# Seven block products in place of eight in a feed-forward layer, with the weight sums on GpSimd

## The chip, the cores and the metric

The kernel runs on one core of a Trainium2 chip. The metric is the device time of one execution, in microseconds (us). A core has TensorE (matmuls into PSUM), VectorE, ScalarE and GpSimd, each with a queue of its own that is worked off in order, and DMA queues that move data between the memory (HBM) and the on-chip SBUF. SBUF and PSUM have 128 partitions; "128x512" is 128 partitions of 512 columns.

## What is computed

One layer: a mixer (a gated delta net and an RWKV7 group), cross attention to a memory, and a feed-forward part, for 256 tokens of width 2048 in float32. The change touches the last part alone:

```python
def squared_relu_mlp(u, w1, w2):
    return jnp.square(jax.nn.relu(u @ w1)) @ w2

# in reference(): w1 is [2048, 8192], w2 is [8192, 2048]
        h = h + squared_relu_mlp(rmsnorm(h, ffn_norm_w[l]), ffn_w1[l], ffn_w2[l])
    return rmsnorm(h, final_norm_w)
```

## The kernel before

Every large product is made of three products of `float32r` parts: an operand x is split into `hi` (a cast, on ScalarE) and `lo = x - hi` (a subtraction, on VectorE), and hi·hi + hi·lo + lo·hi stands for the float32 product. Activations are split once; weights are streamed from HBM, 512 KB at a time, through SP's queue into a ring of five `raw` tiles, and split on the way (`weights`, line 228): `A.copy(hi, w)` on line 239 and the subtraction through the helper on line 110, into three pairs of buffers `whi`/`wlo` (128x512 each).

The feed-forward part (line 1180 on) runs in four chunks `ch` of 2048 hidden columns. In each chunk the first product comes first: `gemm_T` (line 261) computes it transposed, in parts of 128 hidden columns by 256 tokens. A part has 16 k tiles, for each a matmul with a stationary `whi` over 512 columns (both parts of the activations side by side, line 273) and one with `wlo` over 256 columns (line 272 or 275), alternating, all into one PSUM bank. There are 64 such parts. `relu2` then copies one half of the bank (ScalarE), adds the other (VectorE), applies the squared ReLU (VectorE) and splits the result into `fhi` and `flo`.

Then the chunk's second product: `gemm` (line 244), four blocks of 512 output columns, each with 16 k tiles by two halves of the tokens (`m`) by three matmuls of 512 columns (lines 254 to 256). The result is added to `h`, times the squared norm factor `rf`, by `add_ffn` on VectorE. The last block of the last chunk runs one half of the tokens after the other (`gemm_rows`, line 205), so that the first half's final norm (`final`) can go under the second half's matmuls.

GpSimd does nothing in this part but the two powers of the final norm. `tt` (line 110) is `tensor_tensor`, on VectorE unless `e=G` puts it on GpSimd; `stt` (line 113) is `scalar_tensor_tensor` on VectorE. The program's order on each engine is set by a scheduler at build time from the order and priorities of the code; loads and splits of weights have a higher priority.

PSUM has eight banks: three under the tag `g`, two each under `s0` and `s1`, one under `x`. In the feed-forward part only `g` is used.

Of the kernel before, what the change touches and what calls it, by code (L numbers as in the profile page):

```python
# [17 lines left out]
P = 128  # L18
# [22 lines left out]
def host_layout(inp):  # L41
# [32 lines left out]
    def col(v):  # L74
# [22 lines left out]
        "w1": blocks_T(a["ffn_w1"][0]), "w2": blocks(a["ffn_w2"][0]),  # L97
# [7 lines left out]
def body(ctx, tc, I, out, dbg=None, upto=99):  # L105
# [65 lines left out]
    # derived per-channel scalars  # L171
# [15 lines left out]
    def lhs_split(raws, wname, pool, tag):  # L187
        """raw^T (times the norm's weight) split in two float32r parts, four k tiles a tile, as they are asked for."""
# [16 lines left out]
    def gemm_rows(lhs, wblk, evac, kbs, his, los):  # L205
        """the same, the first 128 tokens before the others, from weights that all stay."""
        kbs, w = list(kbs), []
        for m in range(2):
            acc = bank("g")
            for i, kb in enumerate(kbs):  # L210
                if m == 0:
                    with tc.high_priority(3000):
                        raw = wp.tile([P, KB, NB], F32, tag="raw", name=nm("raw"))
                        nc.sync.dma_start(out=raw, in_=wblk[kb])
                        hi, lo = his(), los()
                        A.copy(hi, raw)
                        tt(lo, raw, hi.bitcast(F32), ALU.subtract)
                    w.append((hi, lo))
                hi, lo = w[i]
                for q in range(KB):  # L220
                    first, last = i == 0 and q == 0, i == len(kbs) - 1 and q == KB - 1
                    xh, xo = lhs(kb * KB + q, m)
                    T.matmul(acc, lhsT=xh, rhs=hi[:, q], start=first, stop=False)
                    T.matmul(acc, lhsT=xh, rhs=lo[:, q], start=False, stop=False)
                    T.matmul(acc, lhsT=xo, rhs=hi[:, q], start=False, stop=last)  # L225
            evac(m, acc)

    def weights(src, a, b, parts):
        """a block of weights [128, a, b] in two float32r parts."""
# [14 lines left out]
    def gemm(lhs, wblk, n, evac, kbs=None):  # L244
        """[256 tok, n] = lhs^T @ W: three float32r products stand for the float32 one."""
# [15 lines left out]
    def gemm_T(rhs, wblk, evac):  # L261
        """(x W)^T in four parts of 128 columns, [128 col, (W x_hi, W_hi x_lo)]; rhs(kt) is (x_hi, x_lo)^T, 512 wide."""
        for j in range(4):
            acc = bank("g")
            for b in range(2):
                w = weights(wblk[j, b], 8, P, 2)
                for k in range(8):
                    first, last = b == 0 and k == 0, b == 1 and k == 7
                    x = rhs(8 * b + k)
                    xf = x.rearrange("p a t -> p (a t)")  # L270
                    if not first:
                        T.matmul(acc[:, 0:S], lhsT=w[k][1], rhs=x[:, 0], start=False, stop=False)  # L272
# [26 lines left out]
    def rms(src, name):  # L299
        """1 / rms of the rows of src[:, m, :]."""  # L300
# [60 lines left out]
    # the clock of the array rises and the functions' table loads while the first operands are on their way  # L361
# [73 lines left out]
    # gates of the deltanet: [tok, chunk, head]  # L435
# [35 lines left out]
    inv = [0]  # L471

    def inverse(B, pool, pool2):
        """B is overwritten with the inverse of I + (its strictly upper part); what lies below its diagonal is zero.

        X12 = -X11 B12 X22 for blocks of 2 to 128, the larger ones on tiles of the array."""
# [11 lines left out]
        def quarters(t, n):  # L488
            """the quarters 11, 12, 22 of the diagonal blocks of 2n: [q, block, row, column]."""
# [94 lines left out]
    def rw_shift(pt, c0, names, blks):  # L584
        """columns c0.. of the projection [tok, col] to shifted [col, tok] tiles of two blocks."""
# [12 lines left out]
    def rw_unit(u, r, k, v):  # L598
# [59 lines left out]
        # bonus * v  # L658
# [8 lines left out]
        # scores  # L667
# [21 lines left out]
        # [tok, .] forms  # L689
# [57 lines left out]
        # group norm, bonus, gate  # L747
# [94 lines left out]
    def dn_unit(g, kq, v2):  # L842
# [6 lines left out]
        # norms per token: [tok, (k/q), chunk, head]  # L849
# [21 lines left out]
        # decays, scores  # L871
# [72 lines left out]
        # norm over the head, times silu(z)  # L944
# [90 lines left out]
    def tok_T(src, wname):  # L1035
        """transposes of src [tok, 2048] (times the norm's weight), split in two parts, four k tiles a step."""
# [85 lines left out]
    def low():  # L1122
        for _ in range(2):
            t = da.tile([P, 2, KB, NB], F32R, tag="kq", bufs=2, name=nm("llo"))
            yield t[:, 0]
            yield t[:, 1]
        for _ in range(4):
            yield fp.tile([P, KB, NB], F32R, tag="llo", bufs=4, name=nm("llo"))

    def high():  # L1130
        for _ in range(4):
            t = lx.tile([P, 2, KB, NB], F32R, tag="lx", name=nm("lhi"))
            yield t[:, 0]
            yield t[:, 1]

    llo, lhi = low(), high()

    def final(m):
        ss = part[:, m, 7:8]
        stt(ss, part[:, m, 4:5], 1.0 / D, part[:, m, 6:7], ALU.mult, ALU.add)  # L1140
        ro = small.tile([P, 1], F32, tag="ro", name=nm("ro"))
        power(ro, ss, -0.5, 1)
        for q in range(4):
            d = h[:, m, q * NB:(q + 1) * NB]
            if q == 3:
                stt(d, d, ro, fw[:, q * NB:], ALU.mult, ALU.mult)
            elif q:
                act(d, d, AF.Copy, scale=ro)
            else:
                ts(d, d, ro, ALU.mult)  # L1150
            (A if q % 2 else nc.sync).dma_start(out=out[m * P:(m + 1) * P, q * NB:(q + 1) * NB], in_=d)

    def add_ffn(gcol):
        def f(m, p):
            d = h[:, m, gcol * NB:(gcol + 1) * NB]
            stt(d, p, rf[:, m:m + 1], d, ALU.mult, ALU.add)
        return f

    def last_h(gcol):
        def f(m, p):  # L1160
            sl = slice(gcol * NB, (gcol + 1) * NB)
            d = h[:, m, sl]
            stt(d, p, rf[:, m:m + 1], d, ALU.mult, ALU.add)
            rms_part(h, part, m, gcol)
            tt(d, d, fw[:, sl], ALU.mult)
        return f

    def last(m, p):
        """the last 512 columns in two halves, so that little is left to do once the second's sum of squares is there."""
        V.tensor_reduce(part[:, m, 5:6], part[:, m, 0:3], axis=AX.X, op=ALU.add)  # L1170
        ts(part[:, m, 5:6], part[:, m, 5:6], 1.0 / D, ALU.mult, EPS, ALU.add)
        for i in range(2):
            d = h[:, m, 3 * NB + i * S:3 * NB + (i + 1) * S]
            stt(d, p[:, i * S:(i + 1) * S], rf[:, m:m + 1], d, ALU.mult, ALU.add)
            junk = ptp.tile([P, S], F32, tag="pt", name=nm("junk"))
            act(junk, d, AF.Square, accum=part[:, m, 3 + i:4 + i])
# [48 lines left out]
```

## Time and profile before

| | |
|---|---|
| median of 3 runs | 1446.87 us (1446.61 to 1447.17) |
| span of the profiled execution | 1442.5 us |
| TensorE busy | 1414.8 us, 98% |
| VectorE busy | 950.1 us, 66% |
| ScalarE busy | 780.8 us, 54% |
| GpSimd busy | 50.6 us, 4% |
| DMA | 252.88 MB, mean 175 GB/s |

The runs' time contains the span and some 4 us around it. Busy times are shares of the span. Matmuls are pipelined: the next starts before the one ahead has ended, and the ends are modelled, so a matmul's price is the distance from its start to the next one's. The same holds to a smaller degree for VectorE.

### The profile page before, as it was taken

The numbers are of one execution on the slowest core, as the hardware profiler recorded it, in microseconds if no ns is written. First come the engines' busy times: TensorE is split into PE (matmuls) and PEld (weight loads), VectorE is DVE, ScalarE is ACT, GpSimd is POOL, SyncE is SP. The second block draws the span as 40 slices with busy tenths as digits, with TensorE's granted clock in tenths as the row PEclk, the third lists the DMA queues.
The fourth block names the chain that finished last, engine by engine and source line by source line (L and its number), as shares of the span: only waits on it lengthen the run. The fifth ranks groups of instructions, "written<-read, shape, count | busy, mean of one in ns | idle before, by whom it ended". The sixth has DMA issues, their size and how long they took to land.

```text
span 1442.5 us, 22496 instructions
## 1 busy us (share of the span) xinstructions
PE 1414.8 (98%) x8284; PEld 1168.9 (81%) x8284; DVE 950.1 (66%) x1799; ACT 780.8 (54%) x1491; POOL 50.6 (4%) x66
## 2 busy tenths in 40 slices
PE   9999999999999989999999999999999999999997
PEld 7877788787876868887788888888888888888886
DVE  7748574869587685767676655666556665566664
ACT  7656454555456454566565544555445554455553
POOL 0010001100010000000000000000000000000000
PEclk9999999999999999999999999999999999999999
DMA  7444433454366464556465556555665555655554
GB/s 281 157 145 152 135 121 112 147 177 144 102 200 207 138 190 146 166 173 212 136 209 186 190 192 197 185 187 189 193 197 186 185 190 194 195 182 187 191 188 146
DMA packets 90688, 252.88 MB, mean 175 GB/s; under 512 B 20673, under 2 KB 29393, under 8 KB 90193
## 3 DMA queue, kind: packets, MB, share of 16 engines
q1 hardware_dynamic: 70304, 243.96, 51.2%
q10 hardware_dynamic: 19920, 6.42, 1.8%
q8 instruction: 65, 1.06, 0.3%
q0 software_dynamic: 352, 1.06, 0.2%
q14 instruction: 47, 0.38, 0.1%
HBM read 244.72 MB, written 6.69 MB: 174 GB/s over the span
## 4 chain that ended last, share of the span: by engine, by line
PE 82%; DMA 7%; DVE 6%; ACT 3%; issue 2%; SPq 0%; POOL 0%; ACTq 0%; POOLq 0%; DVEq 0%
PE ps_g L273 16%; PE ps_g L255 16%; PE ps_g L254 15%; PE ps_g L256 15%; PE ps_g L272 8%; DVE wlo L110 2%; PE ps_s L675 2%; DMA scr<-Sc 1%; DMA xc<-inv 1%; DMA mraw<-in_memT_dram 1%; PE ps_x L312 1%; DMA g<-scr 1%; DVE xtmp L110 1%; DMA junk<-in_mem_dram 1%; PE ps_s L312 1%
## 5 line engine op out<-in xcount | busy, mean ns | idle before, releaser
L110 DVE TENSOR_TENSOR wlo<-raw,whi 128x512 fp32r<-128x512 f32 x848 | 583.3, 691 | 388.1 <-ACT whi L239 386.8
L239 ACT CAST whi<-raw 128x512 fp32r<-128x512 f32 x848 | 523.4, 621 | 489.8 <-DVE wlo L110 203.7
L273 PE MATMUL ps_g<-hhl,whi 128*128 128x512 f32 x1024 | 357.6, 398 | 0.2 <-ACT whi L239 0.2
L272 PE MATMUL ps_g<-hhl,wlo 128*128 128x256 f32 x960 | 269.9, 281 | 0.0
L273 PEld LDWEIGHTS ps_g<-hhl,whi 128*128 128x128 f32 x1024 | 188.4, 188 | 42.5 <-ACT whi L239 0.5
L255 PE MATMUL ps_g<-wlo,xhl 128*128 128x512 f32 x512 | 209.9, 410 | 8.4 <-DVE wlo L110 8.3
L256 PE MATMUL ps_g<-whi,xhl 128*128 128x512 f32 x512 | 202.0, 395 | 0.0
L256 PE MATMUL ps_g<-whi,flo 128*128 128x512 f32 x480 | 186.7, 389 | 0.0
L255 PE MATMUL ps_g<-wlo,fhi 128*128 128x512 f32 x480 | 186.7, 389 | 0.0
L254 PE MATMUL ps_g<-whi,xhl 128*128 128x512 f32 x512 | 180.8, 406 | 3.4 <-ACT whi L239 3.4
L272 PEld LDWEIGHTS ps_g<-hhl,wlo 128*128 128x128 f32 x960 | 181.5, 189 | 2.8 <-ACT hhl L122 0.2
L254 PE MATMUL ps_g<-whi,fhi 128*128 128x512 f32 x480 | 151.3, 389 | 0.0
L255 PEld LDWEIGHTS ps_g<-wlo,xhl 128*128 128x128 f32 x512 | 96.6, 189 | 37.7 <-DVE wlo L110 18.2
L254 PEld LDWEIGHTS ps_g<-whi,xhl 128*128 128x128 f32 x512 | 94.6, 189 | 26.7 <-ACT whi L239 5.9
L256 PEld LDWEIGHTS ps_g<-whi,xhl 128*128 128x128 f32 x512 | 96.7, 189 | 18.8 <-issue 0.7
L255 PEld LDWEIGHTS ps_g<-wlo,fhi 128*128 128x128 f32 x480 | 90.1, 188 | 18.8
L256 PEld LDWEIGHTS ps_g<-whi,flo 128*128 128x128 f32 x480 | 90.1, 188 | 18.7
L254 PEld LDWEIGHTS ps_g<-whi,fhi 128*128 128x128 f32 x480 | 90.1, 188 | 18.6
L113 DVE SCALAR_TENSOR_TENSOR cy<-ps_x,colt,cy 128x255 f32<-128x255 f32 (+2 forms) x72 | 34.2, 476 | 10.9 <-ACT cy L122 10.3
L1191 ACT CAST fhi<-hid 128x256 fp32r<-128x256 f32 x64 | 26.1, 408 | 9.5 <-DVE hid L113 0.8
L113 DVE SCALAR_TENSOR_TENSOR hid<-hid 128x256 f32<-128x256 f32 x64 | 27.2, 425 | 2.2
L113 DVE SCALAR_TENSOR_TENSOR h<-ps_g,rf,h 128x512 f32<-128x512 f32 (+1 forms) x34 | 22.8, 712 | 8.0 <-PE ps_g L225 8.0
(360 smaller groups left out, 1540.7 us busy)
## 6 DMA issues: line engine op xcount, KB each, us to landing
raw<-in_w_dram SPq DMA_DIRECT2D x256, 512.0 KB, 3.5
raw<-in_w_in_dram SPq DMA_DIRECT2D x112, 512.0 KB, 3.5
raw<-in_w_out_dram SPq DMA_DIRECT2D x32, 512.0 KB, 3.5
raw<-in_wk_dram SPq DMA_DIRECT2D x8, 512.0 KB, 3.5
mraw<-in_memT_dram SPq DMA_DIRECT2D x8, 512.0 KB, 3.6
raw<-in_wq_dram SPq DMA_DIRECT2D x8, 512.0 KB, 3.4
raw<-in_wv_dram SPq DMA_DIRECT2D x8, 512.0 KB, 3.7
raw<-in_wo_dram SPq DMA_DIRECT2D x8, 512.0 KB, 3.5
```

Source lines behind the costliest of these rows:

```text
L110: return (e or V).tensor_tensor(o, a, b, op=op)
L113: return V.scalar_tensor_tensor(o, a, s, b, op0=op0, op1=op1)
L239: A.copy(hi, w)
L254: T.matmul(acc[m][:, :n], lhsT=xh, rhs=w[q][0], start=first, stop=False)
L255: T.matmul(acc[m][:, :n], lhsT=xh, rhs=w[q][1], start=False, stop=False)
L256: T.matmul(acc[m][:, :n], lhsT=xl, rhs=w[q][0], start=False, stop=last)
L272: T.matmul(acc[:, 0:S], lhsT=w[k][1], rhs=x[:, 0], start=False, stop=False)
L273: T.matmul(acc, lhsT=w[k][0], rhs=xf, start=first, stop=last)
L312: T.transpose(out=o[:, j * P:(j + 1) * P], in_=a, identity=ident)
L675: T.matmul(bb[hl][:, 256 * i:256 * i + 256], lhsT=BK[hs, j, i, cs], rhs=AR[hs, j, :, cs], start=True, stop=True)
L1191: A.copy(hi[:, j], t)
```

## The change

The second product is cut into quads. A quad is 256 tokens by 256 hidden columns by 1024 output columns, a 2x2 by 2x2 product of blocks of 128x128 and 128x512. Eight block products would give its four output blocks; the Strassen-Winograd scheme takes seven, from sums and differences of blocks. With three matmuls each a quad has 21 matmuls of 512 columns, not 24. There are 64 quads (16 groups `g` of 512 hidden columns, two halves `q`, two halves `p` of the output).

- Left operands (`lefts`): for each group, four sums of 128x256 on GpSimd, then two casts and two subtractions (768 and 1024 columns) into seven blocks.
- Right operands (`rights`): one 1 MB load (two buffers), then three instructions on GpSimd (1024, 512 and 512 columns; each depends on the one ahead), and three casts and three subtractions (1536, 1024 and 1024 columns) into single buffers `bs`, `bt` and `bu`.
- Seven PSUM banks collect the seven products over a visit (a run of quads with the same `p`; there are nine). At its end `add_products` combines them into `h`: a copy on ScalarE and eleven operations of 512 columns on VectorE.
- The first product keeps its 64 parts, but 8 of them come first and the other 56 follow one quad each; they use the single bank `x`. Within a part the eight `hi` matmuls of a half come before its eight `lo` matmuls.
- The final norm is spread over the last two visits. `gemm_rows` goes.

```diff
+    def quads(w):
+        b = w.reshape(w.shape[0] // 512, 2, 2, P, w.shape[1] // 1024, 2, NB)
+        b = b.transpose(0, 2, 4, 3, 1, 5, 6).reshape(-1, 2, w.shape[1] // 1024, P, 4, NB)
+        return np.ascontiguousarray(b[:, :, :, :, [1, 0, 3, 2]])
...
-    def gemm_T(rhs, wblk, evac):
-        for j in range(4):
-            acc = bank("g")
+    def gemm_T(rhs, wblk, evac, js=range(4), tag="g"):
+        for j in js:
+            acc = bank(tag)
             for b in range(2):
                 w = weights(wblk[j, b], 8, P, 2)
                 for k in range(8):
...
+                    T.matmul(acc, lhsT=w[k][0], rhs=rhs(8 * b + k).rearrange("p a t -> p (a t)"),
+                             start=b == 0 and k == 0, stop=False)
+                for k in range(8):
+                    T.matmul(acc[:, 0:S], lhsT=w[k][1], rhs=rhs(8 * b + k)[:, 0], start=False,
+                             stop=b == 1 and k == 7)
             evac(j, acc)
...
-    fp = ctx.enter_context(tc.tile_pool(name="fp", bufs=5, reuse_waits="tile"))
-    fw = fp.tile([P, D], F32, name="fw", bufs=1)
-    A.dma_start(out=fw, in_=I["fnw"].to_broadcast([P, D]))
+    fp = ctx.enter_context(tc.tile_pool(name="fp", bufs=1, reuse_waits="tile"))
...
+    def relu2(base):
+        def f(j, p):
+            t = da.tile([P, S], F32, tag="cy", bufs=2, name=nm("hid"))
+            A.copy(t, p[:, S:])
+            tt(t, p[:, 0:S], t, ALU.add)
+            t2 = t.rearrange("p (a t) -> p a t", a=2)
+            stt(base[:, 2 * (j // 2):2 * (j // 2) + 2, j % 2], t2, 0.0, t2, ALU.max, ALU.mult)
+        return f
+
+    def lefts(g, base):
+        sm_ = fp.tile([P, 4, 2, P], F32, tag="sm", name=nm("sm"))
+        tt(sm_[:, 0], base[:, 0], base[:, 2], ALU.add, e=G)
+        tt(sm_[:, 1], sm_[:, 0], base[:, 1], ALU.subtract, e=G)
+        tt(sm_[:, 2], base[:, 0], base[:, 1], ALU.subtract, e=G)
+        tt(sm_[:, 3], base[:, 3], sm_[:, 1], ALU.subtract, e=G)
+        hi = fp.tile([P, 7, 2, P], F32R, tag="ahi", bufs=3, name=nm("ahi"))
+        lo = fp.tile([P, 7, 2, P], F32R, tag="alo", bufs=3, name=nm("alo"))
+        A.copy(hi[:, 0:3], base[:, 1:4])
+        tt(lo[:, 0:3], base[:, 1:4], hi[:, 0:3].bitcast(F32), ALU.subtract)
+        A.copy(hi[:, 3:7], sm_)
+        tt(lo[:, 3:7], sm_, hi[:, 3:7].bitcast(F32), ALU.subtract)
+        left[g] = (hi, lo)
+
+    def split(src, n, tag):
+        hi = fp.tile([P, n, NB], F32R, tag=tag + "h", name=nm(tag))
+        lo = fp.tile([P, n, NB], F32R, tag=tag + "l", name=nm(tag))
+        A.copy(hi, src)
+        tt(lo, src, hi.bitcast(F32), ALU.subtract)
+        return [(hi[:, i], lo[:, i]) for i in range(n)]
+
+    def rights(src):
+        with tc.high_priority(3000):
+            raw = da.tile([P, 4, NB], F32, tag="kq", bufs=2, name=nm("rawq"))
+            nc.sync.dma_start(out=raw, in_=src)
+            t13 = wp.tile([P, 2, NB], F32, tag="raw", name=nm("t13"))
+            tt(t13, raw[:, 0].unsqueeze(1).to_broadcast([P, 2, NB]), raw[:, 1:3], ALU.subtract, e=G)
+            t24 = wp.tile([P, 2, NB], F32, tag="raw", name=nm("t24"))
+            tt(t24[:, 0], raw[:, 2], t13[:, 0], ALU.subtract, e=G)
+            tt(t24[:, 1], raw[:, 3], t24[:, 0], ALU.subtract, e=G)
+            b11, b22, b21 = split(raw[:, 1:4], 3, "bs")
+            t1, t3 = split(t13, 2, "bt")
+            t2, t4 = split(t24, 2, "bu")
+        return {1: b11, 2: b21, 3: b22, 4: t4, 5: t1, 6: t2, 7: t3}
...
+    def quad(g, q, p, acc, first, last, order, done):
+        r = rights(I["w2"][g, q, p])
+        hi, lo = left[g]
+        for n in order:
+            xh, xl_ = hi[:, LHS[n], q], lo[:, LHS[n], q]
+            T.matmul(acc[n], lhsT=xh, rhs=r[n][0], start=first, stop=False)
+            T.matmul(acc[n], lhsT=xh, rhs=r[n][1], start=False, stop=False)
+            T.matmul(acc[n], lhsT=xl_, rhs=r[n][0], start=False, stop=last)
+            if last:
+                done(n)
...
+        def add(m, c, x):
+            d = h[:, m, 1024 * p + NB * c:1024 * p + NB * (c + 1)]
+            stt(d, x, rf[:, m:m + 1], d, ALU.mult, ALU.add)
...
+    jblock(8)
+    A.dma_start(out=fw, in_=I["fnw"].to_broadcast([P, D]))
+    for v, (p, gs) in enumerate(visits):
+        acc = [None] + [bank(t) for t in ("g", "g", "g", "s0", "s0", "s1", "s1")]
+        after = {len(visits) - 1: after_last, len(visits) - 2: lambda m, c: early(m, 2 + c, c)}.get(v)
+        done = add_products(p, acc, after)
+        for g in gs:
+            for q in range(2):
+                end = g == gs[-1] and q == 1
+                order = (1, 2, 3, 5, 6, 7, 4) if end else (1, 2, 3, 5, 7, 6, 4)
+                quad(g, q, p, acc, g == gs[0] and q == 0, end, order, done)
+                jblock()
```

## Rows read from the trace of the kernel before

**Rows 1.** The page's first part: busy us, share of the span, instructions.

```profile
PE 1414.8 (98%) x8284; PEld 1168.9 (81%) x8284; DVE 950.1 (66%) x1799; ACT 780.8 (54%) x1491; POOL 50.6 (4%) x66
```

**Rows 2.** Feed-forward stage: busy time by engine (instructions), granted clock, DMA share, GB/s.

```profile
728.00:1442.50 714.50, 706.14 (x3561) 598.46 (x3560) 443.22 (x750) 367.00 (x656) 1.80 (x3) 1.00 0.57 187
```

**Rows 3.** Waits, 780 to 1400 us: who waited for whom, total us, times, longest.

```profile
DVE wlo L110 <- ACT whi L239: 233.4, 366, 1.0
...
ACT whi L239 <- PE ps_g L273: 91.8, 166, 0.8
```

**Rows 4.** Timeline of TensorE, both products: start us, us, engine, line, operation.

```profile
800.87 0.40 PE L273 MATMUL ps_g<-hhl,whi 128*128 128x512 f32 x1
...
806.52 0.40 PE L273 MATMUL ps_g<-hhl,whi 128*128 128x512 f32 x1
...
824.40 0.62 PE L254 MATMUL ps_g<-whi,fhi 128*128 128x512 f32 x2
...
825.76 0.62 PE L254 MATMUL ps_g<-whi,fhi 128*128 128x512 f32 x2
```

**Rows 5.** Timeline of TensorE, first stage: five matmuls of 272 columns.

```profile
16.22 0.29 PE L404 MATMUL ps_s<-whi,xhl 128*128 128x272 f32 x1
...
16.72 0.41 PE L402 MATMUL ps_s<-whi,xhl 128*128 128x272 f32 x2
```

**Rows 6.** ScalarE's groups by shape, feed-forward stage: busy us, mean ns, idle before.

```profile
L239 ACT CAST whi<-raw 128x512 fp32r<-128x512 f32 x492 | 305.8, 622 | 314.4 <-DVE wlo L110 178.5 <-PE ps_g L273 106.2 <-PE ps_g L256 29.1
...
L216 ACT CAST lhi<-raw 128x1024 fp32r<-128x1024 f32 x8 | 8.4, 1050 | 5.5 <-DMA raw<-in_w_dram 5.5
```

**Rows 7.** VectorE's groups by shape, the same stage and columns.

```profile
L110 DVE TENSOR_TENSOR wlo<-raw,whi 128x512 fp32r<-128x512 f32 x492 | 340.2, 692 | 249.7 <-ACT whi L239 249.6
L113 DVE SCALAR_TENSOR_TENSOR hid<-hid 128x256 f32<-128x256 f32 x64 | 27.2, 425 | 2.2
...
L113 DVE SCALAR_TENSOR_TENSOR h<-ps_g,rf,h 128x512 f32<-128x512 f32 x30 | 21.0, 743 | 0.0
L110 DVE TENSOR_TENSOR llo<-raw,lhi 128x1024 fp32r<-128x1024 f32 x8 | 9.7, 1223 | 4.4 <-ACT lhi L216 4.4
```

**Rows 8.** Timeline of VectorE, two instructions back to back.

```profile
805.85 0.69 DVE L110 TENSOR_TENSOR wlo<-raw,whi 128x512 fp32r<-128x512 f32 x1
806.46 0.42 DVE L110 TENSOR_TENSOR flo<-hid,fhi 128x256 fp32r<-128x256 f32 x1
```

**Rows 9.** GpSimd's groups by shape, whole span.

```profile
L682 POOL TENSOR_SCALAR_AFFINE_SELECT Sc<-Sc 128x512 f32<-128x512 f32 x32 | 20.5, 640 | 167.9 <-ACT Sc L680 159.3 <-issue 8.2 <-PE ps_g L256 0.4
...
L1214 POOL MEMSET const-float32-0.0<- 128x1 f32 x1 | 0.1, 100 | 0.3 <-issue 0.3
```

**Rows 10.** Timelines of GpSimd and VectorE where their instructions overlap.

```profile
419.50 0.64 POOL L880 TENSOR_SCALAR_AFFINE_SELECT Dm<-Dm 128x512 f32<-128x512 f32 x1 [1.01 <-ACT Dm L122]
419.68 1.00 DVE L110 TENSOR_TENSOR wlo<-raw,whi 128x512 fp32r<-128x512 f32 x1
...
412.68 0.68 DVE L110 TENSOR_TENSOR wlo<-raw,whi 128x512 fp32r<-128x512 f32 x1
412.90 0.95 POOL L880 TENSOR_SCALAR_AFFINE_SELECT Dm<-Dm 128x512 f32<-128x512 f32 x1 [1.01 <-ACT Dm L122]
413.54 0.85 DVE L110 TENSOR_TENSOR wlo<-raw,whi 128x512 fp32r<-128x512 f32 x1
...
292.50 1.28 POOL L682 TENSOR_SCALAR_AFFINE_SELECT Sc<-Sc 128x512 f32<-128x512 f32 x2 [4.10 <-ACT Sc L680]
292.56 0.75 DVE L117 TENSOR_SCALAR pt<-ps_g,rx 128x512 f32<-128x512 f32 x1 [1.14 <-PE ps_g L256]
```

**Rows 11.** The same, beside a power of 8 columns on GpSimd.

```profile
341.05 2.02 POOL L110 TENSOR_TENSOR rs<-vr,pw 128x8 f32<-128x8 f32 x1 [39.07 <-DVE vr L118]
...
341.84 0.68 DVE L110 TENSOR_TENSOR wlo<-raw,whi 128x512 fp32r<-128x512 f32 x1
```

**Rows 12.** Timeline of TensorE: its last matmul.

```profile
1433.96 0.39 PE L225 MATMUL ps_g<-lhi,flo 128*128 128x512 f32 x1
```

More of the change, by code (lines that the diff above doesn't have):

```diff
@@ L203, in lhs_split @@
         return get
-    def gemm_rows(lhs, wblk, evac, kbs, his, los):
-        kbs, w = list(kbs), []
-        for m in range(2):
-            acc = bank("g")
[L210 to L226, printed above, removed]
     def weights(src, a, b, parts):
@@ L1130, in high @@
[L1130 to L1140, printed above, removed]
+    A11, A22, A12, S1, S2, S3, S4 = range(7)
+    left = {}
+    def relu2(base):
[6 more added lines that the diff above has]
+        return f
@@ new lines, in add_products, with tmp, both, done @@
+    def add_products(p, acc, after=None):
+        def add(m, c, x):
+            d = h[:, m, 1024 * p + NB * c:1024 * p + NB * (c + 1)]
+            stt(d, x, rf[:, m:m + 1], d, ALU.mult, ALU.add)
+        u = {}
+        def tmp(n):
+            u[n] = ptp.tile([P, NB], F32, tag="pt", name=nm("u"))
+            return u[n]
+        def both():
+            if 6 in u and 7 in have and 8 not in u:
+                tt(tmp(8), acc[7], u[6], ALU.add)
+                add(0, 1, u[8])
+                if after:
+                    after(0, 1)
+                add(0, 0, u[8])
+        have = set()
+        def done(n):
+            have.add(n)
+            if n == 1:
+                A.copy(tmp(1), acc[1])
+                add(1, 0, acc[1])
+            elif n == 2:
+                add(1, 0, acc[2])
+                if after:
+                    after(1, 0)
+            elif n == 3:
+                add(1, 1, acc[3])
+            elif n == 5:
+                add(1, 1, acc[5])
+                add(0, 1, acc[5])
+            elif n == 6:
+                tt(tmp(6), acc[6], u[1], ALU.add)
+                add(1, 1, u[6])
+                if after:
+                    after(1, 1)
+                both()
+            elif n == 7:
+                both()
+            elif n == 4:
+                add(0, 0, acc[4])
+                if after:
+                    after(0, 0)
+        return done
@@ new lines, in body, with square_sum @@
+    visits = []
+    for i in range(8):
+        for p in ((0, 1) if i % 2 == 0 else (1, 0)):
+            if visits and visits[-1][0] == p:
+                visits[-1][1].extend((2 * i, 2 * i + 1))
+            else:
+                visits.append((p, [2 * i, 2 * i + 1]))
+    fw = fp.tile([P, D], F32, name="fw")
+    def square_sum(m, c, slot):
+        junk = ptp.tile([P, NB], F32, tag="pt", name=nm("junk"))
+        act(junk, h[:, m, c * NB:(c + 1) * NB], AF.Square, accum=part[:, m, slot:slot + 1])
@@ L1153, in add_ffn @@
[L1153 to L1176, printed above, removed]
-        stt(part[:, m, 6:7], part[:, m, 3:4], 1.0 / D, part[:, m, 5:6], ALU.mult, ALU.add)
-        final(m)
@@ L1180, in body @@
[L1180 to L1204 removed]
+            if k == 0:
+                stt(d, d, ro, fw[:, q * NB:(q + 1) * NB], ALU.mult, ALU.mult)
+            elif k == 1:
+                ts(d, d, ro, ALU.mult)
+            else:
+                act(d, d, AF.Copy, scale=ro)
@@ new lines, in after_last, with jblock @@
+            (A if k % 2 else nc.sync).dma_start(out=out[m * P:(m + 1) * P, q * NB:(q + 1) * NB], in_=d)
+    bases = {}
+    nj = [0]
+    def jblock(n=1):
+        for _ in range(n):
+            if nj[0] == 64:
+                return
+            g, j = divmod(nj[0], 4)
+            if j == 0:
+                bases[g] = da.tile([P, 4, 2, P], F32, tag="v2", name=nm("base"))
+            gemm_T(hl, I["w1"][g], relu2(bases[g]), js=(j,), tag="g" if nj[0] < 8 else "x")
+            if j == 3:
+                lefts(g, bases[g])
+            nj[0] += 1
```

63 lines of the change are left out of this document (16 added, 47 removed).

## The prediction

> **What bounds the kernel now.** I read the page's busy shares first: TensorE 98% of the span [rows 1]. A busy TensorE row says little by itself, since the ends of matmuls are modelled, so I then took the feed-forward stage alone, in the table of busy times by stretch: from 728 us to the end TensorE is busy 706 of 714.5 us at granted clock 1.00, the upper level of 2.4 GHz, VectorE 443, ScalarE 367, GpSimd 1.8 [rows 2]. In the list of waits VectorE waits 233.4 us for ScalarE's casts, and ScalarE waits for buffers that TensorE still reads [rows 3]; TensorE waits for nobody there. So its own pace sets the time, and I read that from the timeline, from start to start and not from durations. In the second product six matmuls of 512 columns start in 1.36 us (824.40 to 825.76), 0.2267 us each; in the first product sixteen pairs of 512 and 256 columns take 5.65 us (800.87 to 806.52) [rows 4]. The stage is 64 such parts of the first product and 64 x 24 matmuls of the second: 64 x (5.65 + 24 x 0.2267 = 5.44) = 64 x 11.09 = 710 us, and that is the stage. I call 11.09 us a period; everything below is per period.
>
> **TensorE's side of the change.** Of each 24 matmuls of the second product three go: 64 x 3 x 0.2267 = 43.5 us less, a period of 5.65 + 21 x 0.2267 = 10.41 us. The first product keeps its 32 matmuls but does eight of 512 columns and then eight of 256. No run of 256-column matmuls stands in the trace; the nearest is the run of 272 columns at 0.125 us each, weights loaded for each [rows 5]. Scaled by columns that is 0.118, so 16 x (0.2267 + 0.118) = 5.52 us in place of 5.65; at 0.125 it would be 5.63, and the old order's 5.65 is the other end. I take 5.52: TensorE's period is then 10.28 us.
>
> **ScalarE's side.** Its cast takes 622 ns for 512 columns and 1050 for 1024 [rows 6], thus 0.836 ns a column and 0.19 us fixed. Seven blocks in three casts (1536, 1024, 1024) make 3.58 us, the first product's four casts 2.49, its copy of 256 columns by the same rates 0.40, a quarter of the left operands' two casts 0.47, and one copy in each of nine visits 0.09: 7.0 us of 10.28. It stays hidden.
>
> **VectorE's side.** Its subtraction takes 692 ns for 512 columns, 1223 for 1024 [rows 7]: 1.037 ns a column and 0.16 fixed. The seven weight blocks: 1.75 + 2 x 1.22 = 4.20 us (the four blocks of before: 2.77). The first product's four: 2.77. Its two steps of 256 columns behind each part 2 x 0.425. A quarter of the left operands (768 and 1024 columns): 0.55. Nine visits, each with eleven operations of 512 columns at 0.743: 9 x 11 x 0.743 / 64 = 1.15. Sum 9.5 us; back to back these start 0.61 us apart where one takes 0.69 [rows 8], so some 0.08 of each of ten is hidden and VectorE needs 8.6 us. Alone it would fit under 10.28, barely.
>
> **GpSimd's side.** Each quad puts sums of 1024, 512 and 512 columns on GpSimd, each group of 512 hidden columns four more of 256: 2304 columns a period in four instructions. The trace has no such sum. Its nearest row reads one operand and writes one: 640 ns for 512 columns; a memset of one column takes 0.10 us [rows 9]. So a column costs 1.055 ns beside 0.10 fixed. From below: a second operand costs nothing, 0.4 + 2304 x 1.055 = 2.8 us. From above: two operands cost twice the whole row, 2.5 ns a column, 5.8 us. I take twice the net column, 2.11 ns, since the sum must read two columns where the row reads one: 1024 columns 2.26 us, 512 columns 1.18, and 0.4 + 2304 x 2.11 = 5.26 us. The Trainium skill (GPSIMD Engine Reference, Performance versus the Vector engine) gives 4497 ns for a two-input sum of 2048; by it GpSimd's part would be an estimated 5.06 us or a little more for the extra instructions. No run here shows it so far.
>
> **The two together.** This decides the case. Rows 10 set GpSimd's one-operand selections beside VectorE's subtractions that overlap them. GpSimd's runs from 419.50 to 420.14; the subtraction that starts at 419.68 takes 1.00 us, not 0.69, and ends at 420.68, 0.54 after GpSimd. The next: GpSimd until 413.85, the subtraction until 414.39. Five such pairs stand in the trace, two of them shown; the others end 0.53 or 0.54 us after GpSimd's end as well, and 512 x 1.037 ns is 0.53: the subtraction streamed nothing until GpSimd was through. The other way round, the selection at 412.90 takes 0.95 us where a subtraction from 412.68 was ahead of it. A VectorE operation that reads PSUM goes beside GpSimd in 0.75 us, at 292.56 [rows 10]; that is no more than the 0.743 of one with a PSUM operand elsewhere [rows 7]. Against it: subtractions beside GpSimd's 8-column powers keep 0.68 us, inside a power of 2.02 us [rows 11]; but that instruction has 8 columns to read and computes for the rest. The Trainium skill (SBUF — State Buffer, Who interferes with whom) states this as a rule: a VectorE instruction with two SBUF inputs and a GpSimd instruction that reads SBUF lock each other out for a whole instruction. Rows 10 agree to 0.01 us; were it a shared bandwidth instead, the change would come out at the 1403 us of the first rival.
>
> VectorE's columns with both operands in SBUF are, per period: weights 3584 and 2048, square of the ReLU 256, left operands 448, 3 x 9 x 512 / 64 = 216 in the visits; 6552 x 1.037 = 6.79 us. With GpSimd's 5.26 that is 12.05 us in which only one of the two can run. I add 0.35 us for what is neither shared nor hidden (1.1 us of VectorE's PSUM operations and its gaps of about 0.07): a period of 12.4 us, 2.1 more than TensorE's, 1.3 more than today.
>
> **The sum.** The first eight parts of the first product run alone, 8 x 5.52 = 44.2 us, with VectorE's 3.6 each below them. 56 full periods: 694.4. The last eight quads have no part beside them: 3.72 of subtraction, 4.62 of sums, 0.3: 8 x 8.6 = 69. At the end, VectorE's backlog behind the seventh product adds four operations against before, less the fourth product's matmuls: 2 us, on a tail which is now 8.1 us from the last matmul's start at 1433.96 to the end less 0.4 [rows 12]. Together 808 + 2 against 710: 100 us longer. The profiled execution spans 1442.5 us, and the runs' median is 1446.87, 4.4 above: 1542.5 + 4.4 = **1547 us**.
>
> Edits at nothing: sums that are late hold back ScalarE's cast on its in-order queue, and behind it the first product's casts; I cost that in the second rival. The loads are the same bytes (187 GB/s, DMA share 0.57 [rows 2]); the quad's 1 MB load has two buffers, and on SP's queue the first product's loads stand behind it, a period early either way. Cover gone, 1 MB at that rate is 5.6 us, once. The single bank of the first product is emptied while a quad of 4.8 us runs; without it some 0.8 us. The final norm's load goes from the stage's start to behind the eighth part on ScalarE's queue and is needed only in the last two visits.
>
> **Rivals.**
> (a) GpSimd does not hold VectorE, or is quick enough: TensorE's pace stays the bound. That ends on the other side. 56 x 10.28 + 44.2 + 8 x 5.5 (each of the last quads waits for the single buffer of three blocks: 2.04 of matmuls, 1.48 cast, 1.75 subtraction, handovers) = 664, with the tail 44 us less: **1403 us**. The lock need not be absent: it decides from 64 x + 16 = 710, a period of 10.84, which is 4.05 us of GpSimd with nothing unhidden, 3.7 with my 0.35, that is 1.4 to 1.6 ns a column. For it: the lower bound of 2.8 us, by which 6.79 + 2.8 = 9.6 fits under 10.28, and rows 11. Against: rows 10, and that the sum reads two operands. 24%, between 1395 and 1440.
> (b) More than the sum: VectorE's queue is in order, and a subtraction that waits for a cast, that waits for a sum, holds the ready ones behind it. The three weight buffers are single and the first product's pairs three, so VectorE cannot run far ahead. Half a 1024-column sum each period, 1.2 us, gives 13.6: 64 x 13.6 + 16 = 886, **1623 us**. For: today's VectorE spends nearly all of its idle time in waits for casts, 249.6 of 271 us [rows 2, 7]. Against: quads alternate with parts, so another queue entry is mostly ready. 15%.
> (c) The two prices cancel, a period of 10.8: 1447 us. 4%.
>
> **How the numbers follow.** The forecast has 57%, its own range 1500 to 1590 (GpSimd's column from 1.8 to 2.4 ns, unhidden 0 to 0.7). Slower by over 0.2%, about what a measurement of this kernel can tell from no change: 57 + 15 = 72%; within 4%; faster 24%. The range reaches down to 1398, which leaves out the lowest part of (a), and up to 1630, which leaves out part of (b): under 2 in 10.
>
> **What would show it.** In the profile of after: GpSimd's 1024-column sums at 2.3 us or longer; subtractions far above 0.69 us for 512 columns, with the excess where a sum is running, each ending its streaming time after a sum's end; TensorE idle in the stage, at 10.28 / 12.4 = 83% of its pace, released by VectorE's wlo-like tiles and no DMA; the period 12.4 us between equal matmuls of two quads. It would be wrong if the sums come at 1.5 ns a column or less, or if subtractions keep 0.69 us beside them: then TensorE stays full and the period is 10.3.

## The result and the profile after

The changed kernel takes 1649.25 us (median of four runs, 1647.75 to 1649.7) against 1447.02 us: a ratio of 1.139, 95% interval 1.136 to 1.143. It is 202 us slower; the prediction had 100 us, and its range ended at 1630.

The page of the changed kernel, its busy shares, against [rows 1]:

```profile
span 1647.3 us, 22159 instructions
...
PE 1464.0 (89%) x8092; PEld 1171.0 (71%) x8092; DVE 1287.2 (78%) x1774; ACT 843.3 (51%) x1408; POOL 527.3 (32%) x322
```

192 matmuls are gone, and TensorE is busy for longer, over a longer span. The feed-forward stage alone, busy time by engine, granted clock, DMA share and GB/s as in [rows 2]:

```profile
728.00:1647.30 919.30, 754.01 (x3372) 598.57 (x3372) 779.17 (x726) 429.65 (x577) 478.67 (x259) 0.91 0.41 144
```

The stage takes 919 us in place of 714; TensorE is idle in 165 of them, VectorE busy in 779 where it was in 443, and the DMA share falls from 0.57 to 0.41: the transfers have more room than before. The mean granted clock is 0.91. VectorE's groups by shape for the same stage (busy us, mean ns, idle before), against [rows 7], and then GpSimd's, against [rows 9]:

```profile
L116 DVE TENSOR_TENSOR wlo<-raw,whi 128x512 fp32r<-128x512 f32 x252 | 246.6, 1001 | 84.3 <-PE ps_x L254 74.5 <-PE ps_g L254 6.2 <-issue 2.5
L116 DVE TENSOR_TENSOR bs<-rawq,bs 128x1536 fp32r<-128x1536 f32 x64 | 152.6, 2384 | 19.0 <-ACT bs L1133 19.0
...
L119 DVE SCALAR_TENSOR_TENSOR base<-hid 128x256 f32<-128x256 f32 x64 | 55.7, 871 | 1.6
```

```profile
L116 POOL TENSOR_TENSOR t<-rawq,t 128x512 f32<-128x512 f32 x128 | 224.6, 1755 | 96.3 <-issue 54.7 <-DVE wlo L116 15.7 <-DVE bu L116 10.7
L116 POOL TENSOR_TENSOR t<-rawq 128x1024 f32<-128x1024 f32 x64 | 180.9, 2826 | 242.9 <-DVE wlo L116 206.6 <-DMA rawq<-in_w_dram 20.9 <-DVE bu L116 7.7
```

The subtraction of the first product's weights, unchanged in size, went from 692 to 1001 ns, the squared ReLU from 425 to 871. The 1536-column subtraction takes 2384 where 0.16 + 1536 x 1.037 ns is 1754. One place in the timelines shows how, VectorE's and then GpSimd's:

```profile
1014.55 1.28 DVE L116 TENSOR_TENSOR wlo<-raw,whi 128x512 fp32r<-128x512 f32 x2
1015.75 3.42 DVE L116 TENSOR_TENSOR alo<-sm,ahi 128x1024 fp32r<-128x1024 f32 x1
```

```profile
1015.30 2.78 POOL L116 TENSOR_TENSOR t<-rawq 128x1024 f32<-128x1024 f32 x1 [1.76 <-DVE wlo L116]
```

GpSimd starts at 1015.30 while the second of two subtractions is at work, waits for it and ends at 1018.08. The next subtraction, begun at 1015.75, ends at 1019.17, 1.09 us later, and 1024 columns stream in 1.06: the pattern of [rows 10], now with a sum.

The period I read from the second product's casts, one for each quad. These are ScalarE's casts of quads 8, 52, 58 and 59:

```profile
856.81 1.47 ACT L1133 CAST bs<-rawq 128x1536 fp32r<-128x1536 f32 x1
...
1478.41 1.48 ACT L1133 CAST bs<-rawq 128x1536 fp32r<-128x1536 f32 x1 [0.32 <-PE ps_g L1161]
...
1551.50 1.48 ACT L1133 CAST bs<-rawq 128x1536 fp32r<-128x1536 f32 x1 [0.57 <-DMA rawq<-in_w_dram]
...
1584.38 1.47 ACT L1133 CAST bs<-rawq 128x1536 fp32r<-128x1536 f32 x1 [3.92 <-PE ps_g L1161]
```

The 44 quads from 8 to 52, in 621.6 us, make a period of 14.13 us; the forecast was 12.4. Between quads 58 and 59 stand 32.9 us, in which TensorE waits twice for casts of the last group's left operands (`ahi`):

```profile
1574.94 0.50 PE L1159 MATMUL ps_g<-bs,ahi 128*128 128x512 f32 x1 [3.01 <-ACT ahi L1124]
...
1580.51 0.79 PE L1159 MATMUL ps_g<-bs,ahi 128*128 128x512 f32 x1 [2.60 <-ACT ahi L1126]
```

The last matmul starts at 1633.96, and the tail behind it is 13.3 us, 5 longer than before.

### The profile page after: what moved, and what is told of

The parts are those of the page before. It is cut to its first block, busy times and chain, and to the rows that moved or that the text cites. A ratio compares the mean times of both kernels' runs of the same rounds, so it can differ in the third digit from the quotient of the medians.

```text
span 1647.3 us, 22159 instructions
## 1 busy us (share of the span) xinstructions
PE 1464.0 (89%) x8092; PEld 1171.0 (71%) x8092; DVE 1287.2 (78%) x1774; ACT 843.3 (51%) x1408; POOL 527.3 (32%) x322
## 3 DMA queue, kind: packets, MB, share of 16 engines
q0 software_dynamic: 352, 1.06, 0.2%
## 4 chain that ended last, share of the span: by engine, by line
PE 56%; DVE 21%; DMA 8%; issue 7%; ACT 4%; POOL 3%; SPq 0%; ACTq 0%; DVEq 0%; POOLq 0%
PE ps_x L251 10%; PE ps_g L238 7%; DVE wlo L116 7%; PE ps_g L237 7%; PE ps_g L239 7%; DVE bs L116 4%; PE ps_x L254 4%; DVE bt L116 3%; PE ps_s L1160 3%; DMA rawq<-in_w_dram 3%; POOL t L116 2%; PE ps_s L1161 2%; PE ps_g L1160 2%; ACT bs L1133 2%; PE ps_g L1161 2%
## 5 line engine op out<-in xcount | busy, mean ns | idle before, releaser
L222 ACT CAST whi<-raw 128x512 fp32r<-128x512 f32 x608 | 370.6, 619 | 351.7 <-PE ps_x L251 151.3
L251 PE MATMUL ps_x<-hhl,whi 128*128 128x512 f32 x896 | 259.0, 425 | 36.0 <-DVE hid L116 35.3
L116 POOL TENSOR_TENSOR t<-rawq 128x1024 f32<-128x1024 f32 x64 | 180.9, 2826 | 242.9 <-DVE wlo L116 206.6
L116 POOL TENSOR_TENSOR t<-rawq,t 128x512 f32<-128x512 f32 x128 | 224.6, 1755 | 96.3 <-issue 54.7
L251 PEld LDWEIGHTS ps_x<-hhl,whi 128*128 128x128 f32 x896 | 180.4, 208 | 82.4 <-DVE hid L116 44.4
L116 DVE TENSOR_TENSOR bs<-rawq,bs 128x1536 fp32r<-128x1536 f32 x64 | 152.6, 2384 | 19.0 <-ACT bs L1133 19.0
L254 PEld LDWEIGHTS ps_x<-hhl,wlo 128*128 128x128 f32 x896 | 133.6, 197 | 13.6
L254 PE MATMUL ps_x<-hhl,wlo 128*128 128x256 f32 x896 | 136.1, 288 | 0.0
L1133 ACT CAST bs<-rawq 128x1536 fp32r<-128x1536 f32 x64 | 94.4, 1475 | 64.4 <-PE ps_g L1161 48.4
L116 DVE TENSOR_TENSOR bt<-t,bt 128x1024 fp32r<-128x1024 f32 x64 | 100.2, 1566 | 0.5 <-ACT bt L1133 0.5
L1133 ACT CAST bt<-t 128x1024 fp32r<-128x1024 f32 x64 | 67.1, 1048 | 47.4 <-POOL t L116 31.8
```

Source lines behind the costliest of these rows:

```text
L116: return (e or V).tensor_tensor(o, a, b, op=op)
L251: T.matmul(acc, lhsT=w[k][0], rhs=rhs(8 * b + k).rearrange("p a t -> p (a t)"), start=b == 0 and k == 0, stop=False)
L254: T.matmul(acc[:, 0:S], lhsT=w[k][1], rhs=rhs(8 * b + k)[:, 0], start=False, stop=b == 1 and k == 7)
L1133: A.copy(hi, src)
```

## The experiments

Two theories stood against each other. Theory 1: GpSimd's sums and VectorE's subtractions of two SBUF operands exclude each other, and the sum of their times sets the period. Theory 2: the order of the in-order queues and the scarce buffers set it, the sums being one more step of a chain. Each variant was timed once, beside the kernel before on the same chip (1442 to 1454 us, so some 10 us between two variants say little). "Period" is from quad 8 to quad 52, read as above; the expectations have 13.8 and 10.95 us for the first two rows, by another reading.

| kernel | time, us | period, us |
|---|---|---|
| changed kernel | 1649 | 14.13 |
| e1 no sums | 1464 | 11.25 |
| e2 sums on VectorE | 1570 | 12.92 |
| e3 GpSimd writes only | 1498 | 11.91 |
| e4 subtractions with one operand | 1497 | 11.90 |
| e5 five pairs | 1597 | 13.19 |
| e7 no sums, five pairs | 1423 | 10.42 |
| e8 old order of the first product | 1634 | 13.84 |
| e9 own tiles for the sums | 1659 | 14.46 |
| e10 sums on VectorE, five pairs | 1476 | 11.13 |
| e11 one operand, five pairs | 1421 | 10.38 |
| e12 first sums only, five pairs | 1487 | 11.33 |

**e1, no sums.**

```diff
...
-        tt(sm_[:, 0], base[:, 0], base[:, 2], ALU.add, e=G)
...
+        sm_ = base
...
-            t13 = wp.tile([P, 2, NB], F32, tag="raw", name=nm("t13"))
-            tt(t13, raw[:, 0].unsqueeze(1).to_broadcast([P, 2, NB]), raw[:, 1:3], ALU.subtract, e=G)
...
+            t13, t24 = raw[:, 0:2], raw[:, 2:4]
```

> The changed kernel without GpSimd's sums: the blocks are cast and subtracted as they were loaded, and the hidden activations likewise, so the outputs are not the layer's; loads, casts, subtractions and matmuls keep their number. Theory 1 (sums and two-operand subtractions exclude each other): VectorE needs 8.6 us a period and TensorE 10.4, so the period of the feed-forward stage falls from 13.8 us to 10.4 to 10.9 and the time to 1405 to 1440 us. Theory 2 (what costs is the order of the in-order queues and the single weight buffers, with the sums only one step of a chain): the rest of the chain stays, the period is 12 us or more and the time 1500 us or more.

1463.66 us. 186 us go with the sums, so they are most of it. But neither number was met: without any sum the change is still 22 us slower than the kernel before on that chip, at a period of 11.25 us where TensorE needs 10.4. Something of theory 2 is there as well.

**e2, the sums on VectorE.**

```diff
...
-            tt(t24[:, 0], raw[:, 2], t13[:, 0], ALU.subtract, e=G)
...
+            tt(t24[:, 0], raw[:, 2], t13[:, 0], ALU.subtract)
...
```

> The same sums, all on VectorE. Theory 1: VectorE's 8.6 us grow by 2304 columns at 1.037 ns and four fixed parts to some 11.3, nothing is locked out, the period is 11.3 to 12 us and the time 1465 to 1520 us: much faster than with the sums on GpSimd although VectorE has more to do. Theory 2: the chain load, sum, cast, subtraction is as long as before and its sums now queue behind other VectorE work: 1600 us or more.

1569.98 us, between the two: 79 us faster than on GpSimd, though VectorE has 2.7 us more to do in a period, but 50 us above theory 1's upper end. Again a part that theory 1 doesn't explain.

**e3, GpSimd writes but doesn't read.**

```diff
...
-            tt(t13, raw[:, 0].unsqueeze(1).to_broadcast([P, 2, NB]), raw[:, 1:3], ALU.subtract, e=G)
+            for _ in range(3):
+                G.memset(t13, 0.0)
...
-            tt(t24[:, 0], raw[:, 2], t13[:, 0], ALU.subtract, e=G)
-            tt(t24[:, 1], raw[:, 3], t24[:, 0], ALU.subtract, e=G)
+            for _ in range(3):
+                G.memset(t24, 0.0)
```

> GpSimd writes zeros in place of each quad's sums, three times over each of the two tiles, and twice over the left operands' sums, so that it is busy for about as long as with the sums (some 6 us a period) and the casts wait for it as before, but it reads nothing; the outputs are not the layer's. Theory 1: without reads on GpSimd the subtractions keep their 0.69 us for 512 columns, the period is 10.4 to 11 us and the time 1405 to 1450 us. Theory 2: GpSimd's time in the chain is what counts and stays: 1600 us or more.

1497.66 us, 48 over theory 1's upper end and far below theory 2's 1600. GpSimd is busy for 270 of 520 us (780 to 1300), 278 in the changed kernel, and the subtractions are back at 689 ns for 512 columns, here over the whole span:

```profile
L116 DVE TENSOR_TENSOR wlo<-raw,whi 128x512 fp32r<-128x512 f32 x608 | 412.2, 689 | 286.8 <-ACT whi L222 138.2
```

**e4, one operand.** The other side of the pair: the sums stay, the subtractions read one operand.

```diff
-                tt(lo, w, hi.bitcast(F32), ALU.subtract)
+                if wide[0]:
+                    V.tensor_reduce(lo, hi.bitcast(F32).unsqueeze(3), axis=AX.X, op=ALU.add)
...
-        tt(lo, src, hi.bitcast(F32), ALU.subtract)
+        V.tensor_reduce(lo, hi.bitcast(F32).unsqueeze(3), axis=AX.X, op=ALU.add)
...
```

> GpSimd's sums stay as they are, but VectorE's subtractions in the feed-forward part become reductions over an axis of one element, which read the cast alone: one SBUF operand, as many columns, the same place in the chain; the outputs are not the layer's. Theory 1: the sums no longer hold them (only the squared ReLU and three operations of a visit still read two), GpSimd's 6.0 us fit beside VectorE's 8.6, the period is 10.4 to 11.2 us and the time 1405 to 1465 us. Theory 2: same chain, same buffers, 1600 us or more.

1496.52 us, within 1.2 us of e3. VectorE's groups, 857 to 1300 us, first of e4 and then of the changed kernel:

```profile
L225 DVE TENSOR_REDUCE wlo<-whi 128x512 fp32r<-128x512 f32 x153 | 99.9, 678 | 51.3 <-PE ps_x L258 51.3
```

```profile
L116 DVE TENSOR_TENSOR wlo<-raw,whi 128x512 fp32r<-128x512 f32 x127 | 123.0, 991 | 47.8 <-PE ps_x L254 47.4 <-issue 0.3
```

Whether GpSimd stops reading SBUF or VectorE reads one operand less, the stretched instructions are gone and 152 us with them. So the two engines' reads get in each other's way, shown from both sides; that they exclude each other is for e6 to show. The reductions also no longer read the loaded tiles, which come free earlier; e3, where the subtractions still read them, ends at the same time, so that is not what gives the 152 us. What is left, 1497 against an expected 1405 to 1465, is the same gap as in e1 and 33 us more. The idle time in both rows names TensorE's line 254 (258 in e4), the matmuls on the `lo` parts: VectorE waits for one of the three buffer pairs of the first product's weights.

**e6, the pairs alone.** A kernel that runs each instruction alone and then in pairs on both engines.

> A small kernel that computes none of the layer: VectorE's subtraction (128x512, two SBUF operands), its form with one operand in PSUM and a one-operand reduction, GpSimd's sum of 1024 columns (plain and with a repeated first operand) and of 512, and GpSimd's zeros, first each alone, then in pairs on both engines at once, 16 of VectorE's beside 4 (or 8) of GpSimd's. Theory 1 (they exclude each other for whole instructions): 16 subtractions beside 4 sums take the sum of both times alone, 16 x 0.60 + 4 x 2.4 to 2.8 = 19 to 21 us; beside zeros, and with a PSUM operand or a single operand beside sums, VectorE keeps 0.60 us an instruction and the pair takes the longer of the two, 10 to 12 us. If the two shared the port by turns within an instruction, the first pair would take 11 to 15 us and both engines' instructions would be longer. The repeated operand costs 0.4 us of the 2.8 that the 1024-column sum took in the changed kernel, or the sum is longer than two of 512 by itself.

VectorE's and GpSimd's groups by shape (names: `va` and `ga` to `gd` alone; `vg` subtractions beside sums, `pg` with an operand in PSUM beside sums, `vw` subtractions beside zeros, `rg` reductions beside sums):

```profile
L54 DVE TENSOR_TENSOR vg_ov<-vg_a,vg_b 128x512 f32<-128x512 f32 x16 | 19.2, 1197 | 47.2 <-ACT vg_b L43 46.7
...
L54 DVE TENSOR_TENSOR vw_ov<-vw_a,vw_b 128x512 f32<-128x512 f32 x16 | 11.1, 692 | 3.5 <-ACT vw_b L43 3.0
L55 DVE TENSOR_TENSOR pg_ov<-acc,pg_b 128x512 f32<-128x512 f32 x16 | 11.1, 691 | 5.0 <-ACT pg_b L43 4.5
L56 DVE TENSOR_REDUCE rg_ov<-rg_b 128x512 f32<-128x512 f32 x16 | 11.0, 686 | 5.0 <-ACT rg_b L43 4.4
L54 DVE TENSOR_TENSOR va_ov<-va_a,va_b 128x512 f32<-128x512 f32 x8 | 5.5, 692 | 20.7 <-ACT va_b L43 20.4
```

```profile
L57 POOL TENSOR_TENSOR vg_og<-vg_a,vg_b 128x1024 f32<-128x1024 f32 x4 | 10.8, 2694 | 3.8 <-ACT vg_b L43 3.6
...
L57 POOL TENSOR_TENSOR ga_og<-ga_a,ga_b 128x1024 f32<-128x1024 f32 x4 | 9.4, 2340 | 30.5 <-ACT ga_b L43 30.3
L58 POOL TENSOR_TENSOR gb_og<-gb_a,gb_b 128x1024 f32<-128x1024 f32 x4 | 9.4, 2339 | 4.7 <-ACT gb_b L43 4.5
...
L59 POOL TENSOR_TENSOR gc_og<-gc_a,gc_b 128x512 f32<-128x512 f32 x4 | 5.0, 1262 | 4.7 <-ACT gc_b L43 4.5
```

VectorE's timeline, the sixteen subtractions beside sums and the sixteen with an operand in PSUM:

```profile
72.95 19.67 DVE L54 TENSOR_TENSOR vg_ov<-vg_a,vg_b 128x512 f32<-128x512 f32 x16 [46.73 <-ACT vg_b L43]
97.08 11.57 DVE L55 TENSOR_TENSOR pg_ov<-acc,pg_b 128x512 f32<-128x512 f32 x16 [4.47 <-ACT pg_b L43]
```

The sixteen subtractions beside four sums take 19.67 us from first start to last end; sixteen with a PSUM operand beside as many sums take 11.57, and four sums alone 9.59. Side by side it would be the longer of the two, 11.6; one after the other it is 21.2 with every fixed part, and 16 x 0.531 + 4 x 2.34 = 17.9 for the streaming and the sums alone. The measured time lies between these two, far from shared use. Beside zeros, with a PSUM operand or with a single operand the mean stays at 686 to 692 ns. The sum costs (2340 - 1262) / 512 = 2.105 ns a column beside 0.18 us; a repeated operand costs nothing. So the sum of 1024 columns at 1015.30, with its 2.78 us, took 0.44 more than alone, as it had to wait for the subtraction directly ahead.

**e5, five pairs.** Two more pairs for the first product's weights, in the place of the final norm's weights.

```diff
+                extra = wide[0] is not None and wide[1] % 5 >= 3
+                wide[1] += 1
+                pool, nb, tg = (wide[0], 2, "x") if extra else (wp, WB, "w")
-                hi = wp.tile([P, n, b], F32R, tag="whi", bufs=WB, name=nm("whi"))
+                hi = pool.tile([P, n, b], F32R, tag=tg + "hi", bufs=nb, name=nm("whi"))
...
-    fw = fp.tile([P, D], F32, name="fw")
+    wide[:] = [fp, 0]
...
```

> The changed kernel with five pairs of split first-product weights in its feed-forward stage in place of three; their place comes from the final norm's weights, which are left out (constants stand for them, and their load goes), so the outputs are not the layer's. Theory 1 with the in-order queue: VectorE is idle 1.9 us of each period of 13.85, 1.3 of them because TensorE still holds a pair; with five the period falls to 12.5 to 13.1 and the time to 1565 to 1605 us. Theory 1 alone (the exclusion sets the pace, idle time is filled otherwise): 1635 to 1650 us.

1597.06 us, as the in-order queue had it, with a period just above its range. Busy times, 857 to 1300 us, of the changed kernel and then of five pairs:

```profile
857.00:1300.00 443.00, 377.08 (x1696) 302.19 (x1696) 373.98 (x347) 209.62 (x274) 231.50 (x128) 0.91 0.44 152
```

```profile
857.00:1300.00 443.00, 380.14 (x1781) 310.10 (x1779) 439.41 (x362) 214.46 (x286) 262.33 (x134) 0.95 0.46 160
```

VectorE is busy in 374 of 443 us with three pairs, in 439 with five: 99%, its blocked time counted; before its `wlo` subtractions it waited 47.4 us for a pair with three, and 0.2 us in all with five. From there VectorE's own work and the time in which GpSimd blocks it set the pace, 13.19 us.

**e7, no sums and five pairs** (the edits of e1 and e5).

> Both: no sums on GpSimd and five pairs. Theory: of the 58 us by which the kernel without sums missed TensorE's pace the pairs are the larger part; the period falls from 10.95 to 10.4 to 10.6 us and the time from 1464 to 1420 to 1440 us. If the single weight buffers of the second product are what costs: 1455 us or more.

1423.13 us, period 10.42. Of the 58 us of e1 41 are the pairs (1463.66 - 1423.13); the rest was not there to be had, since 10.42 is TensorE's own pace.

**e8, the old order of the first product.**

```diff
-                for k in range(8):
                     T.matmul(acc[:, 0:S], lhsT=w[k][1], rhs=rhs(8 * b + k)[:, 0], start=False,
                              stop=b == 1 and k == 7)
```

> The changed kernel with the first product's matmuls in the old alternating order. The hi part is then held longer and the lo part is wanted earlier and given back earlier. If it is the grouping that holds the lo parts and so VectorE (1.3 us of idle time a period): 1580 to 1620 us. If grouping was a help, since it lets TensorE begin a part before VectorE has the lo parts: 1650 to 1700 us.

1634.31 us, neither of the two: by these two numbers the grouping costs 15 us with three pairs, where two pairs more give 52.

**e9, own tiles for the sums.**

```diff
-            t13 = wp.tile([P, 2, NB], F32, tag="raw", name=nm("t13"))
+            t13 = fp.tile([P, 2, NB], F32, tag="t13", name=nm("t13"))
...
-    fw = fp.tile([P, D], F32, name="fw")
...
```

> The changed kernel, three pairs, with the two tiles of the quad's sums taken out of the ring that the first product's loads use and given buffers of their own (one each); their place comes from the final norm's weights as with five pairs (constants stand for them, the outputs are not the layer's), so it is also the control for that. In the changed kernel the first product's loads wait on SP for those tiles. If that coupling costs: 1590 to 1625 us. If the pairs were the bottleneck and not the loads: 1635 to 1655 us.

1658.90 us, 4 above the second range, and 1.141 times the kernel before on that chip, where the change has 1.139. The ring that loads and sums share is not what costs, and leaving the final norm's weights out gives nothing (unless the two cancel, which was not tried apart): e5's gain is the pairs.

**e10, the sums on VectorE and five pairs** (the edits of e2 and e5).

> The sums on VectorE and five pairs (the final norm's weights are constants, as there). With three pairs it took 1570 us, a period of 12.9 us, though VectorE has work for 11.3. If the missing 1.6 us are again the pairs: a period of 11.3 to 11.9 and 1465 to 1510 us, far below the 1597 us of the sums on GpSimd with five pairs. If VectorE's in-order queue costs it as much with any number of buffers: 1540 us or more.

1475.90 us, period 11.13, where 11.3 was VectorE's work (it is busy for 442.93 of 443 us). With five pairs the same sums cost 121 us less on VectorE than on GpSimd.

**e11, one operand and five pairs** (the edits of e4 and e5).

> GpSimd's sums as in the change, five pairs, and one-operand reductions in place of the subtractions (the outputs are not the layer's). Nothing but the exclusion differs from the 1597 us of five pairs with subtractions. Theory: with the lock gone the sums fit beside VectorE and the time is that of five pairs without sums, 1423, up to 1450 us. If the sums cost through the chain as well: 1470 us or more.

1420.96 us, period 10.38, with all of GpSimd's sums in it:

```profile
857.00:1300.00 443.00, 443.00 (x2263) 377.04 (x2262) 366.11 (x460) 281.44 (x369) 246.00 (x173) 1.00 0.56 204
```

GpSimd is busy for 246 us beside a VectorE that is busy for 366, in a stretch in which TensorE never stands. Against e5 the number of SBUF operands in VectorE's subtractions differs, and with it how early the loaded tiles come free; but in e5 VectorE is busy or blocked for 439 of 443 us, so tiles that come earlier could give it next to nothing. The exclusion costs 1597.06 - 1420.96 = 176 us, and with it gone the sums cost nothing (e7: 1423.13).

**e12, the first sums only, five pairs** (beside e5's edits).

```diff
...
-            t24 = wp.tile([P, 2, NB], F32, tag="raw", name=nm("t24"))
-            tt(t24[:, 0], raw[:, 2], t13[:, 0], ALU.subtract, e=G)
-            tt(t24[:, 1], raw[:, 3], t24[:, 0], ALU.subtract, e=G)
+            t24 = raw[:, 2:4]
...
```

> Five pairs, and of the quad's sums GpSimd makes the first, of 1024 columns, alone; the two of 512 are left out (the outputs are not the layer's). It takes 2.5 of GpSimd's 5.3 us from the period of 13.2. Exclusive use: 6.8 us of two-operand columns and 2.8 to 3.0 of sums fit under TensorE's 10.4, with 0.4 to 1.1 unhidden a period of 10.4 to 11.0, and 1425 to 1460 us. If it is not the sum of the two times that counts but the number of times that they meet: half of the way, about 1510 us.

1487.35 us, above the first range and below the second number: the period is 11.33, 0.9 over TensorE's pace, although 6.8 us of two-operand columns and 3.0 of sums fit under it. So exclusive use that fits under TensorE's pace is not free. VectorE is busy in 421 of 443 us: its own work and the time in which it is blocked together nearly fill its queue.

Only e7 and e11 end below the kernel before, one without the sums, one without the second operands. Some 1421 us is what seven products would give with five pairs if the sums were free.

## Why the prediction was wrong

The direction was right, and so was the mechanism that it put first, the exclusion. A second one, the scarce pairs, stood only among the rivals, and the size was half of what was measured.

- **TensorE's pace**: 10.28 us a period forecast, 10.38 to 10.42 measured where nothing else binds (e11, e7). The grouped part of the first product takes 5.60 us, not 5.52 (in the changed kernel's first parts eight-matmul runs start at 746.19 and 751.79), hardly less than the 5.65 of [rows 4]. The 1403 us of rival (a) became 1421 and 1423.
- **GpSimd's price**: 2.11 ns a column was worked out from a one-operand row by doubling; e6 has 2.105. The fixed part was too small, 0.10 us from a memset where e6 has 0.18, so a period's four sums cost 4 x 0.18 + 2304 x 2.105 = 5.57 us and not 5.26. 4497 ns for 2048 columns in the Trainium skill (GPSIMD Engine Reference, Performance versus the Vector engine) agrees: e6's two prices give 0.18 + 2048 x 2.105 = 4.5 us.
- **The exclusion**: [rows 10] held for sums too, shown from both sides by e3, e4 and e11 and by itself in e6. The Trainium skill's rule (SBUF — State Buffer, Who interferes with whom) agrees in all four forms: two SBUF operands against a reading GpSimd 1197 ns, against a writing one 692, one operand in PSUM 691, a reduction 686.
- **The step that failed is "I add 0.35 us for what is neither shared nor hidden."** With e6's price of the sums the exclusive use is 6.79 + 5.57 = 12.36 us, 0.31 more than forecast; what came on top was 1.77 us, not 0.35, in 14.13 us. With five pairs it is 0.83 us (e5). I had let nearly all of VectorE's other work, 8.6 - 6.8 = 1.8 us of PSUM operations and fixed parts, run under GpSimd's sums. The 8.6 are right: in e7 VectorE is busy for 365.35 of 443 us, 8.6 of each 10.42. In e5 it was hardly ever free: 13.19 = 8.6 of its own and 4.6 of GpSimd's 5.57, so only 1.0 us of the sums' time was used for something else. e12 says the same with less GpSimd.
- The other 0.94 us is **rival (b)'s mechanism**: an in-order VectorE that cannot run ahead with three pairs. I priced it at 1623 us and gave it 15%, for a sum that holds up the queue; e5, e7 and e10 show that it is the pairs, in every variant: 52, 41 and 94 us (with the sums on GpSimd, without, on VectorE). It could have been suspected ahead: ScalarE waited for TensorE's hold on these pairs 91.8 us [rows 3], which cost nothing while VectorE had a third of its time free. The change filled that third.
- **The last eight quads** were costed at 69 us as if the operands were there. From the cast of quad 56 at 1522.05 to the last matmul's start at 1633.96 pass 112 us. Quads 58 and 59 need the last group's left operands, and between their casts stand 32.9 us of last part, squared ReLU, sums, casts and subtractions in a row; the lead of eight parts is used up there. With five pairs that step is 8.2 us, and without sums it is 21.6 with three pairs and 6.5 with five (e1, e7), so it too hangs on the pairs.
- In sum: a period's missing 1.73 us are 0.94 of the pairs, 0.48 that did not hide and 0.31 of GpSimd's price; 44 of them make 76 us. Some 40 come at the end (quad 52's cast to the end of the span takes 168.9 us, where four periods, 69 and a tail of 10 were forecast), and the start is some 9 us faster (134.6 us from the stage's first matmul at 722.2 to the cast of quad 8, against 44.2 + 8 x 12.4): 107, where 105 were missing.

What stays open: how the 0.83 us of e5 divide between fixed parts, PSUM operations and the hand-over, and how much of the time the lower clock (below) costs. Neither was tried.

## What to carry to other kernels

Here work on GpSimd left VectorE's instructions at their length where these read at most one operand from SBUF (e6, e11) or where GpSimd only wrote (e3, e6). Where VectorE reads two and GpSimd reads as well, add GpSimd's time to VectorE's, and hide nothing of VectorE's other work under the sum unless a row shows it. A change that takes work from the bounding engine and fills the next one turns buffers that were just enough into waits: look, before it is made, which waits of the next engine were free of charge and price them in. One experiment that changes only the number of operands (a reduction in place of a subtraction) tells interference from latency in a single run.

## What was not expected of the hardware

TensorE's clock fell in stalls that were short. After 3.52 us without work the next eight matmuls of 512 columns, from 1009.47 on, took 2.87 us from the first start to the next matmul's, at a granted clock of 0.65 on average, so in part at the lower level; the same eight take 1.82 at 1.00 when TensorE comes from work. After 5.9 us without work it ran at 0.50, the lower level of 1.2 GHz, for the next 4.4 us. The stretches of the changed kernel (busy times as above, granted clock), and then TensorE's row with the first stall:

```profile
1009.47:1012.34 2.87, 2.87 (x9) 2.28 (x9) 1.97 (x2) 1.80 (x3) 2.35 (x4) 0.65 0.80 248
1021.46:1023.28 1.82, 1.82 (x10) 1.50 (x9) 1.13 (x2) 1.82 (x2) 1.43 (x2) 1.00 0.00 0
1606.35:1610.78 4.43, 4.43 (x10) 3.48 (x11) 4.43 (x5) 1.47 (x1) 1.07 (x1) 0.50 0.70 237
```

```profile
1009.47 3.08 PE L251 MATMUL ps_x<-hhl,whi 128*128 128x512 f32 x8 [3.52 <-DVE hid L116]
```

So a stage that no longer keeps TensorE full can also make it slower when it does work; what that cost here was not measured. Also: GpSimd was not starved by sixteen subtractions issued back to back. Four sums beside them ended 11.01 us after their start (9.59 alone), and it was VectorE that lost the time.
